# Routing steps of the second and third dense tile moved between the gate blocks of the tile in front

## The chip, the cores and the metric

The kernel runs on one core of a Trainium2 chip. The metric is the device time of one execution in microseconds (us). The engines named below are PE (TensorE, matrix products), DVE (VectorE), ACT (ScalarE), POOL (GpSimd, which here issues the gathers of table rows) and SP (SyncE, which issues the other transfers). Each engine runs its own list of instructions strictly in order; an instruction that has to wait for another engine or for a transfer holds up everything that is queued behind it on its engine.

## What is computed

One decoder layer on 512 tokens of width 1024: convolution and differential attention side by side, an output projection, then an expert layer ("peer"), then a gated per-layer embedding and a last norm. The change is in the expert layer, which for every token scores 128 + 128 keys in each of 8 heads, keeps the 16 best pairs, and mixes the 128 experts that these pairs name out of 16384:

```python
s = einsum('thcd,cnd->thcn', q, keys)
sv, si = top_k(s, 16)                       # per head and half
cand = sv[:, :, 0, :, None] + sv[:, :, 1, None, :]
cs, ci = top_k(cand.reshape(T, 8, 256), 16)
e1 = take_along_axis(si[:, :, 0], ci // 16); e2 = take_along_axis(si[:, :, 1], ci % 16)
experts, gates = e1 * 128 + e2, softmax(cs)
u = u_tab[experts]; h = gelu(einsum('cd,ckd->ck', x, u)) * gates
y = einsum('ck,ckd->cd', h, v_tab[experts])
```

## The kernel before

The 512 tokens are four tiles of 128. Three of them (the dense tiles, t = 0, 1, 2; `NA` = 3) compute all 16384 experts and multiply by a matrix of gates that is zero where an expert was not chosen. The fourth tile (the sparse tile) gathers its 128 u rows and then its 128 v rows per token from memory.

**Ups.** The dense tiles need u for 128 chunks of 128 experts. `up(c)` (L595) loads a chunk, splits it into a high part (`uhi`, ACT, L600) and a low part (`ulo`, a subtraction on DVE, L601; the first four on POOL), runs 24 matmuls (L67 to L69) and applies gelu (`av`, ACT). The third matmul of an up is the first that needs `ulo`. `more(n)` issues the next n ups. Ups are counted from 0 here; "up 48" is the 49th.

**Routing of a dense tile.** `pairs` (L504) finds the 16 best pairs of four heads, on DVE; it is called twice for a tile. `decode` (L515) turns them into two expert coordinates (one pass of the loop over c each) and the gates (`ef`). `decodeA` (L554) then transposes `ef` on PE (L558) and copies it on ACT (L559 to L562, the last is `gTH`) and DVE (`gTL`, L563).

**Gate blocks.** For every 16 tokens of a dense tile one block (L672 to L705) builds one-hot matrices on DVE (`o1` L690, on ACT in every third block; `eq2` L694; `o2` L695 and L696), multiplies them on PE (32 matmuls, L702) and copies the result out on ACT (`stage`, L704). Eight blocks make a tile. After every second block the gates are written to memory (`g_spill`).

**Rows.** `sparse(i)` (L573) gathers row i for each token of the sparse tile (a POOL issue, L576, 512 KB) into one of four buffers (`row`, L571), and DVE multiplies and sums it (L579). The DVE instruction is kept in program order. After 32 rows ACT applies gelu (`bh`, L582) and DVE multiplies by the gates (L583). `rows(n)` issues the next n.

**Order.** The program text gives the ups, rows and blocks in the order of the loop at L663: for each dense tile first two calls of `pairs` with two rows after each, then `decodeA`, two rows, four ups, then eight times three ups (`PER`), four rows (`ROWS`) and a block. A scheduler then reorders instructions on each engine by its own forecast, except those that are kept in program order. What is left over of the ups and rows is done in the last loop (L801), which runs the products with v (`down`, L740) for 128 chunks.

Of the kernel before, what the change touches and what calls it, by code (L numbers as in the profile page):

```python
# [10 lines left out]
F32 = mybir.dt.float32  # L11
# [15 lines left out]
NH, NK, TOPK = 8, 128, 16  # L27
HC = 2 * NH
NA = 3
# [7 lines left out]
HG = 4  # L37
WARM = 12
MIX = 2
EMB = 8  # L40
FIRST, PER = 16, 3
ROWS, POOLED = 4, 4
ACT_EVERY = 3
GS = 16384.0
# [10 lines left out]
def hymba_layer(ctx: ExitStack, tc: tile.TileContext, I, out):  # L55
# [270 lines left out]
    for i in range(len(units) + MIX + 1):  # L326
        if i < len(units):
            h, t = units[i]
# [5 lines left out]
        if 0 <= i - MIX - 1:  # L334
            h, t = units[i - MIX - 1]
# [134 lines left out]
    rbp = tc.alloc_tile_pool(name="rbp", bufs=1, side="right", reuse_waits="tile")  # L470
# [10 lines left out]
    setA, setB = store(rt, NA), store(rbp, 1)  # L481
# [30 lines left out]
        for j in range(HG):  # L512
            top16(cand[:, j], cs[:, t, h + j], ci[:, t, h + j], NCAND)

    def decode(st, t):  # L515
        sv, si, cs, ci = st
        ef = rbp.tile([128, 3, NH * TOPK], F32, name="ef")
        s16 = rbp.tile([128, 2, TOPK, NH], F16, name="s16")
        V.tensor_copy(s16, si[:, t].rearrange("p h c j -> p c j h"))
        late, fa, fb = (rbp.tile([128, TOPK, NH], F32, name="dc%d" % i) for i in range(3))  # L520
        iu = rbp.tile([128, NH, TOPK], U32, name="iu")
        iv = iu.rearrange("p h k -> p k h")
        V.tensor_scalar(late, ci[:, t].rearrange("p h k -> p k h"), float(NC0), None, op0=OP.is_ge)
        for c in range(2):
            if c == 0:
                V.tensor_scalar(iu, ci[:, t], 4, None, op0=OP.logical_shift_right)
                V.tensor_copy(fa, iv)
                V.tensor_scalar(iu, ci[:, t], 2, None, op0=OP.logical_shift_right)
                V.scalar_tensor_tensor(fb, iv, -12.0, fa, op0=OP.add, op1=OP.subtract)
            else:  # L530
                V.tensor_scalar(iu, ci[:, t], 15, None, op0=OP.bitwise_and)
                V.tensor_copy(fa, iv)
                V.tensor_scalar(iu, ci[:, t], 3, None, op0=OP.bitwise_and)
                V.tensor_tensor(fb, iv, fa, op=OP.subtract)
            V.tensor_tensor(fb, fb, late, op=OP.mult)
            fi = rbp.tile([128, TOPK, NH], F16, name="fi")
            V.tensor_tensor(fi, fa, fb, op=OP.add)
            eq = rbp.tile([128, TOPK, TOPK, NH], F16, name="eq")
            ev = eq.rearrange("p j k h -> p j (k h)")
            V.tensor_tensor(ev, jrep, fi.rearrange("p k h -> p (k h)")[:, None, :].to_broadcast([128, TOPK, 128]), op=OP.is_equal)  # L540
            V.tensor_tensor(eq, eq, s16[:, c][:, :, None, :].to_broadcast([128, TOPK, TOPK, NH]), op=OP.mult)
            for n in (8, 4, 2):
                V.tensor_tensor(ev[:, 0:n], ev[:, 0:n], ev[:, n:2 * n], op=OP.add)
            V.tensor_tensor(ef[:, c], ev[:, 0], ev[:, 1], op=OP.add)
        gt = rbp.tile([128, NH, TOPK], F32, name="gts")
        V.tensor_tensor(gt, cs[:, t], cs[:, t, :, 0:1].to_broadcast([128, NH, TOPK]), op=OP.subtract)
        A.activation(gt, gt, AF.Exp)
        gs = rbp.tile([128, NH], F32, name="gs")
        V.tensor_reduce(gs, gt, axis=AX.X, op=OP.add)
        V.reciprocal(gs, gs)  # L550
        V.tensor_tensor(ef[:, 2].rearrange("p (k h) -> p h k", h=NH), gt, gs[:, :, None].to_broadcast([128, NH, TOPK]), op=OP.mult)
        return ef

    def decodeA(t):  # L554
        ef = decode(setA, t)
        tp = rbank()
        for c in range(3):
            T.transpose(tp[:, c * 128:c * 128 + 128], ef[:, c], ident)  # L558
        A.activation(ne1[:, t], tp[:, 0:128], AF.Copy, scale=-1.0)  # L559
        A.activation(e1T[:, t], tp[:, 0:128], AF.Copy)  # L560
        A.activation(e2T[:, t], tp[:, 128:256], AF.Copy)
        A.activation(gTH[:, t], tp[:, 256:384], AF.Copy, scale=GS)  # L562
        V.scalar_tensor_tensor(gTL[:, t], tp[:, 256:384], GS, gTH[:, t], op0=OP.mult, op1=OP.subtract)  # L563

    def routeB():
        ef = decode(setB, 0)
        V.tensor_copy(bgate, ef[:, 2])
        V.scalar_tensor_tensor(bidx, ef[:, 0], float(NK), ef[:, 1], op0=OP.mult, op1=OP.add)

# [57 lines left out]
    def more(n):  # L627
        nonlocal nu
        while n > 0 and nu < EARLY:
            up(first[nu])  # L630
            nu += 1
            n -= 1
# [21 lines left out]
    def rows(n):  # L654
        nonlocal nxt
        while n > 0 and nxt < 128:
            sparse(nxt)
            nxt += 1
            n -= 1

    routeB()
    more(FIRST)
    for t in range(NA):  # L663
        for h in range(0, NH, HG):
            pairs(setA, t, h)
            rows(2)
        decodeA(t)
        rows(2)
        more(4)
        for b in range(128 // GT):  # L670
            stage = gst.tile([128, NK, GT], F32, name="stage")
            for g in range(GT // GB):  # L672
                tk = b * GT + g * GB
                more(PER)
                rows(ROWS)
                sh = [128, GB // 2, 128, 2]

# [251 lines left out]
```

## Time and profile before

| what | value |
|---|---|
| median of 3 runs | 1567.97 us (1564.33 to 1573.69) |
| the profiled execution | 1570.4 us, its span 1568.6 us |
| mean granted clock of TensorE | 0.983 |
| PE busy | 1505.2 us (96%) |
| DVE busy | 1248.0 us (80%) |
| ACT busy | 719.7 us (46%) |
| POOL busy | 465.7 us (30%) |

The profile gives each instruction's start and duration, and for an engine that sat idle what ended the idle time. Routing, ups and gate blocks run from about 367 us to 879 us of the span; what comes before (attention and convolution) and most of what comes after (the products with v) is not touched. The durations of neighbours on DVE overlap a little, so for a sum the distance from one start to the next is what counts.

### The profile page before, as it was taken

The numbers are of one execution on the slowest core, as the hardware profiler recorded it, in microseconds if no ns is written. First come the engines' busy times: TensorE is split into PE (matmuls) and PEld (weight loads), VectorE is DVE, ScalarE is ACT, GpSimd is POOL, SyncE is SP. The second block draws the span as 40 slices with busy tenths as digits, with TensorE's granted clock in tenths as the row PEclk, the third lists the DMA queues.
The fourth block names the chain that finished last, engine by engine and source line by source line (L and its number), as shares of the span: only waits on it lengthen the run. The fifth ranks groups of instructions, "written<-read, shape, count | busy, mean of one in ns | idle before, by whom it ended". The sixth has DMA issues, their size and how long they took to land. (4 is left out here: it accounts for less than half of the span.)

```text
span 1568.6 us, 22429 instructions
## 1 busy us (share of the span) xinstructions
PE 1505.2 (96%) x7929; PEld 1315.7 (84%) x7929; DVE 1248.0 (80%) x2411; ACT 719.7 (46%) x1133; POOL 465.7 (30%) x316
## 2 busy tenths in 40 slices
PE   8989898999999999999999999999999999998997
PEld 6867476889999989999999878888888888876786
DVE  4999863789999999988884677878788787768756
ACT  5434664223347764776666433333333333334433
POOL 0000103331223444344442234433344453432000
PEclk9999998999999999999999999999999999999999
DMA  7232245311779999999999999999998898989612
GB/s 238 94 109 54 81 161 204 107 55 41 256 211 347 336 339 335 349 400 373 363 366 361 351 345 332 329 328 329 332 338 328 308 326 307 325 325 329 232 40 81
DMA packets 148689, 410.31 MB, mean 262 GB/s; under 512 B 15072, under 2 KB 66144, under 8 KB 147040
## 3 DMA queue, kind: packets, MB, share of 16 engines
q1 hardware_dynamic: 111136, 272.55, 49.9%
q0 software_dynamic: 36864, 134.23, 22.8%
q10 hardware_dynamic: 576, 2.10, 0.3%
q8 instruction: 62, 1.02, 0.3%
q14 instruction: 51, 0.42, 0.1%
HBM read 355.41 MB, written 51.31 MB: 259 GB/s over the span
## 5 line engine op out<-in xcount | busy, mean ns | idle before, releaser
L576 POOL DMA_INDIRECT row<-in_v,bidx x128 | 214.8, 1678 | 300.8 <-DVE acc L587 285.1
L576 POOL DMA_INDIRECT row<-in_u,bidx x128 | 193.8, 1514 | 345.4 <-DVE row L579 301.0
L69 PE MATMUL ups<-mTH,ulo 128*128 128x384 f32 x760 | 256.7, 338 | 2.3 <-DVE ulo L601 2.2
L67 PE MATMUL ups<-mTH,uhi 128*128 128x384 f32 x760 | 257.9, 339 | 0.3 <-ACT av L607 0.3
L68 PE MATMUL ups<-mTL,uhi 128*128 128x384 f32 x760 | 256.3, 337 | 0.0
L740 PE MATMUL y<-vlo,hH 128*128 128x512 f32 x768 | 238.5, 392 | 11.2 <-DVE vlo L64 11.2
L600 ACT ACTIVATE uhi<-uraw 128x1024 fp32r<-128x1024 f32 x128 | 135.2, 1060 | 229.3 <-PE ups L68 157.0
L740 PE MATMUL y<-vhi,hH 128*128 128x512 f32 x768 | 237.9, 391 | 2.3 <-ACT vhi L63 2.3
L740 PE MATMUL y<-vhi,hL 128*128 128x512 f32 x768 | 237.6, 391 | 0.0
L63 ACT ACTIVATE hH<-hf 128x384 fp32r<-128x384 f32 x128 | 67.1, 524 | 288.9 <-PE y L740 215.9
L601 DVE TENSOR_TENSOR ulo<-uraw,uhi 128x1024 fp32r<-128x1024 f32 x124 | 150.8, 1221 | 44.0 <-ACT uhi L600 40.8
L740 PEld LDWEIGHTS y<-vlo,hH 128*128 128x128 f32 x768 | 143.6, 188 | 45.6 <-DVE vlo L64 15.7
L579 DVE SCALAR_TENSOR_TENSOR row<-row,mB 128x1024 f32<-128x1024 f32 x128 | 152.4, 1223 | 25.2 <-DMA row<-in_u,bidx 25.0
L740 PEld LDWEIGHTS y<-vhi,hH 128*128 128x128 f32 x768 | 143.7, 188 | 32.3 <-ACT vhi L63 4.0
L740 PEld LDWEIGHTS y<-vhi,hL 128*128 128x128 f32 x768 | 144.7, 188 | 30.3
L587 DVE SCALAR_TENSOR_TENSOR acc<-row,bh,acc 128x1024 f32<-128x1024 f32 x127 | 162.5, 1279 | 0.0
L64 DVE TENSOR_TENSOR hL<-hf,hH 128x384 fp32r<-128x384 f32 x128 | 71.3, 557 | 112.8 <-ACT hH L63 112.8
L64 DVE TENSOR_TENSOR vlo<-vraw,vhi 128x1024 fp32r<-128x1024 f32 x128 | 156.2, 1220 | 5.3 <-ACT vhi L63 5.3
L69 PEld LDWEIGHTS ups<-mTH,ulo 128*128 128x128 f32 x760 | 142.6, 188 | 3.7 <-DVE ulo L601 3.6
L67 PEld LDWEIGHTS ups<-mTH,uhi 128*128 128x128 f32 x760 | 142.7, 188 | 1.4 <-ACT av L607 0.6
L68 PEld LDWEIGHTS ups<-mTL,uhi 128*128 128x128 f32 x760 | 142.7, 188 | 1.0
L63 ACT ACTIVATE vhi<-vraw 128x1024 fp32r<-128x1024 f32 x128 | 135.6, 1059 | 15.8 <-DMA vraw<-in_v 15.3
(276 smaller groups left out, 2613.5 us busy)
## 6 DMA issues: line engine op xcount, KB each, us to landing
uraw<-in_ut SPq DMA_DIRECT2D x128, 512.0 KB, 6.6
vraw<-in_v SPq DMA_DIRECT2D x128, 512.0 KB, 5.5
g_spill<-stage SPq DMA_DIRECT2D x12, 2048.0 KB, 10.4
gt<-g_spill SPq DMA_DIRECT2D x16, 1536.0 KB, 11.5
a_spill<-av SPq DMA_DIRECT2D x101, 192.0 KB, 6.8
ga<-a_spill SPq DMA_DIRECT2D x101, 192.0 KB, 6.9
qraw<-in_wq SPq DMA_DIRECT2D x16, 512.0 KB, 3.8
wraw<-in_w_in SPq DMA_DIRECT2D x15, 512.0 KB, 4.1
```

The lines of the kernel that those rows point to most:

```text
L63: A.activation(hi, src, AF.Copy)
L64: V.tensor_tensor(lo, src, f32(hi), op=OP.subtract)
L67: T.matmul(ps, wh, xh, start=first, stop=False)
L68: T.matmul(ps, wh, xl, start=False, stop=False)
L69: T.matmul(ps, wl, xh, start=False, stop=last)
L576: P.indirect_dma_start(out=row, out_offset=None, in_=I["u"] if i < 128 else I["v"], in_offset=bass.IndirectOffsetOnAxis(ap=bidx[:, j:j + 1 ...
L579: tc.keep_in_program_order(V.scalar_tensor_tensor(row, row, 1.0, mB, op0=OP.mult, op1=OP.mult, accum_out=ba[:, j:j + 1]))
L587: tc.keep_in_program_order(V.scalar_tensor_tensor(acc, row, bh[:, j:j + 1], acc, op0=OP.mult, op1=OP.add))
L600: A.activation(hi, raw, AF.Copy)
L601: (P if c in first[:POOLED] else V).tensor_tensor(lo, raw, f32(hi), op=OP.subtract)
L740: T.matmul(y[t][n], w[:, sl], x[:, n * 512:n * 512 + 512], start=c == 0 and w is hH and x is hi, stop=c == NK - 1 and l)
```

## The change

The routing of a dense tile becomes a generator, `routeA`, that stops after each call of `pairs`, after each of the two coordinates, and after the gates; its last step is the transposes and copies. That makes six steps. The routing of tile 0 still runs as a whole before the first block, now with two rows and one up (`CHORE_UPS`) at each of its five stops. The routing of tile t + 1 is stepped once in each of the first six blocks of tile t, behind the three ups of the block and ahead of its four rows; in the last two blocks nothing is left to step. Ahead of tile 1 and tile 2 stand four ups and no rows; ahead of tile 0 the four ups are gone (five were issued at the stops).

```diff
+CHORE_UPS = 1
...
-    def decode(st, t):
+    def decode(st, t, ef):
         sv, si, cs, ci = st
-        ef = rbp.tile([128, 3, NH * TOPK], F32, name="ef")
...
             V.tensor_tensor(ef[:, c], ev[:, 0], ev[:, 1], op=OP.add)
+            yield
...
-        return ef
-
-    def decodeA(t):
-        ef = decode(setA, t)
+        yield
+
+    def new_ef():
+        return rbp.tile([128, 3, NH * TOPK], F32, name="ef")
+
+    def routeA(t, paired=False):
+        for h in range(0, 0 if paired else NH, HG):
+            pairs(setA, t, h)
+            yield
+        ef = new_ef()
+        yield from decode(setA, t, ef)
         tp = rbank()
...
     def routeB():
-        ef = decode(setB, 0)
+        ef = new_ef()
+        for _ in decode(setB, 0, ef):
+            pass
...
     routeB()
     more(FIRST)
+    chores = routeA(0)
     for t in range(NA):
-        for h in range(0, NH, HG):
-            pairs(setA, t, h)
+        for _ in chores:
             rows(2)
-        decodeA(t)
-        rows(2)
-        more(4)
+            more(CHORE_UPS)
+        if t:
+            more(4)
+        chores = routeA(t + 1) if t + 1 < NA else iter(())
         for b in range(128 // GT):
             stage = gst.tile([128, NK, GT], F32, name="stage")
             for g in range(GT // GB):
                 tk = b * GT + g * GB
                 more(PER)
+                next(chores, None)
                 rows(ROWS)
```

The lists of instructions that come out of the scheduler show where this lands. The line numbers of the changed kernel are 8 to 12 higher; `ulo` is the subtraction of an up, `row,ba` one gathered row.

DVE before, from the subtraction of up 43 on, while PE works on the last block of tile 0:

```order
L601 TENSOR_TENSOR ulo<-uraw,uhi 128x1024
L579 SCALAR_TENSOR_TENSOR row,ba<-row,mB 128x1024 x4
L498 MAX_INDEX ci<-cs,tscr 128x8
L494 MAX cs<-cand 128x8
L579 SCALAR_TENSOR_TENSOR row,ba<-row,mB 128x1024
L601 TENSOR_TENSOR ulo<-uraw,uhi 128x1024
L579 SCALAR_TENSOR_TENSOR row,ba<-row,mB 128x1024 x2
L601 TENSOR_TENSOR ulo<-uraw,uhi 128x1024
L579 SCALAR_TENSOR_TENSOR row,ba<-row,mB 128x1024
```

Here eight rows stand close together, numbers 34 to 41. The rows 30 to 33 stand ten and more microseconds of DVE work ahead of them, and the instruction `gTL` of tile 1 follows only behind up 46.

DVE after, from `gTL` of tile 1 on, which now stands behind the subtraction of up 41:

```order
L571 SCALAR_TENSOR_TENSOR gTL<-rbank,gTH 128x128
L589 SCALAR_TENSOR_TENSOR row,ba<-row,mB 128x1024 x2
L702 TENSOR_TENSOR o_5488<-irep,e1T 128x2048
L593 TENSOR_TENSOR bh<-bh,bgate 128x32
L589 SCALAR_TENSOR_TENSOR row,ba<-row,mB 128x1024 x4
L611 TENSOR_TENSOR ulo<-uraw,uhi 128x1024
L589 SCALAR_TENSOR_TENSOR row,ba<-row,mB 128x1024 x2
L611 TENSOR_TENSOR ulo<-uraw,uhi 128x1024
L707 TENSOR_TENSOR o_5491<-eq_5490,gTH 128x2048
L611 TENSOR_TENSOR ulo<-uraw,uhi 128x1024
L589 SCALAR_TENSOR_TENSOR row,ba<-row,mB 128x1024 x4
L708 TENSOR_TENSOR o_5491<-eq_5490,gTL 128x2048
```

One more subtraction and four more rows follow: rows 30 to 45, sixteen of them, now stand between the subtractions of up 41 and up 46, and none stands between up 35 and up 41.

ACT before, at the copies of the transposed `ef` of tile 1 (L559 to L562); `stage` is the copy out of a gate block, here the last of tile 0:

```order
L600 ACTIVATE uhi<-uraw 128x1024
L607 ACTIVATE av<-ups 128x384
L704 ACTIVATE stage<-rbank 128x4x128 x4
L559 ACTIVATE ne_2154<-rbank 128x128
L560 ACTIVATE e1T<-rbank 128x128
L561 ACTIVATE e2T<-rbank 128x128
L562 ACTIVATE gTH<-rbank 128x128
```

ACT after, at the same copies:

```order
L610 ACTIVATE uhi<-uraw 128x1024
L617 ACTIVATE av<-rbank 128x384
L567 ACTIVATE ne_2154<-rbank 128x128
L568 ACTIVATE e1T<-rbank 128x128
L569 ACTIVATE e2T<-rbank 128x128
L570 ACTIVATE gTH<-rbank 128x128
L716 ACTIVATE stage<-rbank 128x4x128 x4
L592 ACTIVATE bh<-ba 128x32
L610 ACTIVATE uhi<-uraw 128x1024
```

The copies moved from behind the eighth block of tile 0 to ahead of its sixth, five ups earlier, and the gelu of the first 32 row products (`bh`) follows the copies of that block at once.

## Rows read from the trace of the kernel before

**Rows 1.** Busy time by stretch; columns PE, PEld, DVE, ACT, POOL, PEclk, DMA share, GB/s

```profile
560.00:580.00 20.00, 17.06 (x113) 16.57 (x114) 17.11 (x43) 14.05 (x25) 9.65 (x7) 0.95 0.96 348
580.00:600.00 20.00, 17.93 (x90) 17.61 (x89) 19.83 (x43) 11.80 (x20) 6.69 (x5) 0.88 1.00 388
...
375.00:600.00 225.00, 214.95 (x1370) 210.08 (x1369) 215.24 (x520) 128.91 (x196) 70.47 (x48) 0.98 0.82 288
600.00:860.00 260.00, 260.00 (x1830) 257.46 (x1829) 216.28 (x272) 174.30 (x265) 107.55 (x70) 1.00 0.97 362
860.00:935.00 75.00, 70.77 (x336) 61.63 (x336) 49.46 (x73) 27.34 (x39) 23.55 (x15) 0.98 0.98 361
...
1100.00:1200.00 100.00, 100.00 (x463) 85.59 (x462) 78.61 (x91) 37.34 (x50) 41.89 (x25) 1.00 0.93 335
```

**Rows 2.** PE's waits from 375 to 620 us: total us, times, longest

```profile
PE rbank L69 <- DVE ulo L601: 7.8, 6, 2.9
PE ups L69 <- DVE ulo L601: 2.2, 3, 0.9
```

**Rows 3.** PE in order of time: start, us, what, idle before

```profile
428.70 0.44 PE L69 MATMUL rbank<-mTH,ulo 128*128 128x384 f32 x1 [1.30 <-DVE ulo L601]
466.40 2.01 PE L702 MATMUL rbank<-o,o 128*128 128x128 f16 x32
468.22 0.42 PE L67 MATMUL rbank<-mTH,uhi 128*128 128x384 f32 x1
578.12 0.69 PE L69 MATMUL rbank<-mTH,ulo 128*128 128x384 f32 x1 [2.92 <-DVE ulo L601]
594.59 0.44 PE L69 MATMUL rbank<-mTH,ulo 128*128 128x384 f32 x1 [2.07 <-DVE ulo L601]
600.43 0.33 PE L69 MATMUL ups<-mTH,ulo 128*128 128x384 f32 x1
604.59 0.33 PE L69 MATMUL ups<-mTH,ulo 128*128 128x384 f32 x1
```

**Rows 4.** DVE in order of time, from up 14 to up 48

```profile
427.43 1.21 DVE L601 TENSOR_TENSOR ulo<-uraw,uhi 128x1024 fp32r<-128x1024 f32 x1
508.56 1.23 DVE L579 SCALAR_TENSOR_TENSOR row<-row,mB 128x1024 f32<-128x1024 f32 x1 [2.05 <-DMA row<-in_u,bidx]
543.50 1.22 DVE L601 TENSOR_TENSOR ulo<-uraw,uhi 128x1024 fp32r<-128x1024 f32 x1
544.63 1.22 DVE L695 TENSOR_TENSOR o<-eq,gTH 128x2048 f16<-128x2048 f16 x1
545.77 1.22 DVE L696 TENSOR_TENSOR o<-eq,gTL 128x2048 f16<-128x2048 f16 x1
568.21 1.22 DVE L579 SCALAR_TENSOR_TENSOR row<-row,mB 128x1024 f32<-128x1024 f32 x1
569.36 1.22 DVE L579 SCALAR_TENSOR_TENSOR row<-row,mB 128x1024 f32<-128x1024 f32 x1
575.69 1.23 DVE L579 SCALAR_TENSOR_TENSOR row<-row,mB 128x1024 f32<-128x1024 f32 x1 [2.38 <-DMA row<-in_u,bidx]
598.99 1.22 DVE L601 TENSOR_TENSOR ulo<-uraw,uhi 128x1024 fp32r<-128x1024 f32 x1
```

**Rows 5.** POOL in order of time: the issues of four gathers

```profile
569.71 1.68 POOL L576 DMA_INDIRECT row<-in_u,bidx  x1 [7.79 <-DVE row L579]
571.69 1.99 POOL L576 DMA_INDIRECT row<-in_u,bidx  x1 [0.30 <-issue]
573.99 0.93 POOL L576 DMA_INDIRECT row<-in_u,bidx  x1 [0.30 <-issue]
```

**Rows 6.** The tile `row` from 400 to 600 us: gathers from issue to landing

```profile
DMA to landing us min/median/max: 5.1/8.0/11.1
```

**Rows 7.** PE in order of time: the last gate block, the first product with v

```profile
847.04 1.96 PE L702 MATMUL rbank<-o,o 128*128 128x128 f16 x32
878.58 0.63 PE L740 MATMUL y<-vhi,hH 128*128 128x512 f32 x2
```

**Rows 8.** ACT and DVE in order of time: the first two parts of v

```profile
871.88 1.06 ACT L63 ACTIVATE vhi<-vraw 128x1024 fp32r<-128x1024 f32 x1 [1.91 <-DMA vraw<-in_v]
873.22 1.22 DVE L64 TENSOR_TENSOR vlo<-vraw,vhi 128x1024 fp32r<-128x1024 f32 x1
```

## The prediction

> **What bounds the kernel now.** I read the busy times by stretch first. From 600 to 860 us PE is busy all of the time and its clock is full: there the ups and gate blocks run back to back, and no rearrangement can win anything. From 375 to 600 us PE is idle for 10 of 225 us while DVE is busy for 215 [rows 1]. The list of PE's waits says for what: nine times for `ulo`, the subtraction of an up on DVE, 10.0 us in all [rows 2]. So in this stretch, and only there, DVE is the late one: routing of all three tiles, one-hot matrices, rows and subtractions come to more than PE's own work. The two largest waits, 2.92 and 2.07 us, stand at the border between tile 0 and tile 1 [rows 3].
>
> That lag can be counted. At up 14 PE has just waited for DVE (428.70, subtraction at 427.43), and at up 48 the two meet again (600.43, subtraction at 598.99) [rows 3, 4]. Between them PE has 34 ups and 8 blocks. An up is 4.16 us (600.43 to 604.59), a block 1.82 (466.40 to 468.22) [rows 3]: with 0.6 for six transposes 156.8 us. It took 171.7, so it lost 14.9; that is more than the idle time in its list, because in the last 40 us it also ran at a granted clock of 0.95 and 0.88 [rows 1], which cost nothing of its own, since DVE set the pace. DVE between the same two points has 34 subtractions (1.13 from start to start), 40 rows (1.145), 35 one-hot instructions (1.135) [rows 4]; that is 38.4 + 45.8 + 39.7. Its list of waits in between is six waits for a gathered row, of which 2.05 and 2.38 are the longest [rows 4] and which sum to 6.95, and about 1.8 us in small pieces, 8.7 in all. What is left of its 171.6 us is 38.9 for the short routing instructions. So the loss of 14.9 is 6.1 of DVE work in excess of PE's work (162.8 against 156.8), and 8.7 in which DVE itself stood waiting, nearly all of it for rows. Everything that the change can do here is in these two terms. From about 605 us on PE is never behind again before the products with v begin.
>
> **The change, part by part.**
>
> *Amount of work.* Nothing is added: the same instructions, moved. The rows issued in the tile loop are 10 + 3 x 32 = 106 instead of 3 x (6 + 32) = 114; eight rows go to the last loop. There each is 1.145 us of a DVE that is busy for 78.61 of 100 us while PE is full [rows 1], so they hide. If that cover were gone they would cost 9 us.
>
> *The first term, DVE's excess.* The scheduler had already put much of tile 1's and tile 2's routing between the blocks of the tile in front, so the step-wise text moves less than it says. I add up the list of the changed kernel with the same distances from start to start, again from up 14, up to which both lists are alike. Up to up 42: 28 subtractions, 32 rows, 28 one-hots, 33.7 of routing, 133.7 us against 130.0 of PE (28 ups, 7 blocks): excess 3.8. Up to up 52, where it is largest: 42.9 + 52.7 + 43.1 + 41.5 = 180.3 against 175.2 (38 ups, 9 blocks): 5.0. Up to up 59: 50.9 + 65.3 + 49.9 + 46.5 = 212.6 against 208.1: 4.5. The excess is thus 1.1 us below the 6.1 of before. That is the whole direct gain.
>
> *The second term, DVE's waits for rows.* Rows have four buffers. In a run of rows the fifth can be fetched only when DVE has freed the first. Before: the first row of a run at 568.21 was done when the next began at 569.36, POOL issued the next gather at 569.71, and the row that used it began at 575.69 after a wait of 2.38 us [rows 4, 5], 6.0 us from issue to use. Over the stretch a gather takes 5.1 to 11.1 us, median 8.0 [rows 6]; POOL's next issue follows after 0.93 to 1.99 us plus 0.30 [rows 5]. Before, the longest run was eight rows. Now the rows of block six are held behind `gTL` of tile 1, which waits in program order ahead of them, and the list shows sixteen (rows 30 to 45) between up 41 and up 46, with none in the five ups ahead. Up to the start of the last there are fifteen rows, four subtractions and three one-hots to do, 17.2 + 4.5 + 3.4 and `bh` with 0.1: 25.2 us. The gathers set: 1.5 us to free and issue the first, then eleven more at a spacing of 1.3 to 2.3, then the landing of 6 to 9. With 1.6 and 6 the last is there at 25.1, and only the fifth row waits: four rows, a one-hot and `bh` end at 5.8, the gather at 1.5 + 6, a wait of 1.7 us; with 2.3 and 9 at 35.8, a wait of 10.6. In between, 2.1 and 8 give 32.6 - 25.2 = 7.4; I take 7, nearest to the median landing. Two smaller runs: rows 22 to 29 around up 33 (0 to 4, I take 2) and rows 54 to 60 around up 58 (0 to 3.6, I take 2.5). The small pieces stay at 1.8. So the waits are 10.8 up to up 52 and 13.3 up to up 59, where before they were 8.7.
>
> *The lag then.* At up 52: 5.0 + 10.8 = 15.8. At up 59: 4.5 + 13.3 = 17.8. PE's loss is the largest of these, 17.8, against 14.9: 2.9 us more. With all waits at their low ends (1.7 + 1.8) it is 8.5, a gain of 6.4; with all at their high ends (10.6 + 4 + 3.6 + 1.8 = 20.0) it is 24.5, a loss of 9.6.
>
> *New waits in order.* PE's transposes of tile 1 now stand ahead of its sixth block and want the gates of `decode`; by the same sums DVE is done with these some 20 us before PE gets there, so PE doesn't wait. `gTL` on DVE waits for the copies on ACT; DVE comes there after PE's transposes, since it is the late engine. On ACT the gelu `bh` waits for row 31 and has the `uhi` of up 42 behind it; DVE wants that only after four more rows. I cost all three at nothing; the cover is DVE's lag itself, and without it the first would cost up to 1.8, a block.
>
> *The passage to v.* One up more is issued ahead of the first block, so one fewer (six, not seven) stands between the last block and the first product with v. In that time the last gates go to memory and back. Before, `vhi` was done at 872.94 and `vlo` at 874.44, and PE began at 878.58 [rows 7, 8]: 5.6 and 4.6 us of slack (`vlo` is wanted 0.4 later). An up is 4.16 [rows 3], so 1.5 and 0.4 are left. I take 1 us, from 0 to 3: the transfers of this stretch run at a share of 0.98 [rows 1].
>
> **Sum.** 2.9 + 1 is 3.9 us on the profiled execution's 1570.4, so about 1574.3; the median of the runs shown is 1567.97, and on that base 1572.
>
> **The rivals.**
>
> *The burst costs what the slower gathers say.* If the sixteen rows run at POOL's longer spacing of 2.3 and landings of 9 us and more, the loss is 9.6, with the passage up to 12.6: 1578 to 1581. For it: landings up to 11.1 were seen [rows 6]. Against it: while DVE stands, no other buffers come free and other transfers pause too, and in the burst of before the landing was down to 6.0. It decides from waits of 15 us up to up 59. The Trainium skill (SBUF — State Buffer, section "A bandwidth-pool intuition that's wrong") says that a gather's descriptors can be locked out by a DVE instruction on the shared port, and that an issue of about 0.62 us then takes about 3.1; by that figure, an estimate, eleven issues would add some 9 us more and the time would be near 1590. The issues of this trace take 0.93 and 1.99, so it bears out a slow-down with a busy DVE, but not that size.
>
> *The rows land in time.* If the run is fed at 1.6 us and 6 us, as in the best part of the burst of before, DVE's waits shrink to 3.5, PE's loss is 8.5, and the time is 1562; if the small pieces of 1.8 go too, the loss is 6.7 and the time 1560, and lower only if the passage to v wins as well, some 4 us at most, 1556. For it: rows are spread more evenly at the start of tile 0 (14 instead of 6 by up 21), and the eight-row run at the border is gone. Against it: the list shows a longer run, not a shorter one.
>
> *It does nothing.* The scheduler had hoisted the routing already; then excess and waits trade evenly and the time stays at 1568. This lies inside the forecast's own range, 1563 to 1576.
>
> **How the numbers follow.** 0.5% is 7.8 us, about what a measurement of this kernel can tell from no change: below 1560 is faster, above 1576 slower. Forecast and "does nothing" together have 0.44, all of it within 0.5%. The slow burst has 0.36. The rows in time have 0.20, of which 0.06 lie above 1560 and 0.14 below, since my sums can be off by the few us that part the two. That makes 0.14 faster, 0.50 the same, 0.36 slower. The range reaches up to the end of the slow burst and down to where the fast case leaves it: 1560 to 1582.
>
> **What will show it.** Right: PE's waits for `ulo` still end by about 630 us and come to a loss of 16 to 20 from up 14 on; DVE's waits for rows between up 41 and up 46 are 5 to 9 us, larger than any group before; PE full from 640 to 860; 106 rows done before the first v product. Wrong: PE waiting at the transposes or at a block (L702 before, L714 after); waits for rows below 4 us (then faster); a wait of over 3 us ahead of the first product with v; or a change in the stretch after 935 us, where I expect none.

## The result, and the profile after

The changed kernel takes 1579.45 us (median of 6 runs, 1574.05 to 1582.46) and the kernel before, timed beside it, 1568.89 us (6 runs, 1564.16 to 1573.69). The ratio is 1.0071 with a 95% interval of 1.005 to 1.0092: slower by 0.7%, 10.6 us. The profiled execution took 1579.0 us with a span of 1577.2, 8.6 us over that of before. That lies in the range given (1560 to 1582) and at the time that the rival "the burst costs what the slower gathers say" had (1578 to 1581), not at the forecast. By the prediction's own lines (above 1576 is slower) it is the slower case, to which it gave 0.36, and not the same, to which it gave 0.50.

Busy time by stretch in the profile after (columns as in [rows 1]):

```profile
375.00:600.00 225.00, 212.01 (x1360) 208.65 (x1359) 210.42 (x500) 124.84 (x192) 70.40 (x50) 0.98 0.82 284
600.00:860.00 260.00, 250.62 (x1725) 246.60 (x1724) 205.87 (x262) 168.26 (x258) 94.81 (x59) 0.98 0.89 327
860.00:935.00 75.00, 72.89 (x396) 66.50 (x395) 45.16 (x64) 31.37 (x42) 18.88 (x13) 1.00 0.99 359
560.00:580.00 20.00, 14.55 (x96) 14.08 (x96) 11.86 (x18) 13.10 (x26) 10.02 (x8) 0.83 0.95 340
580.00:600.00 20.00, 17.86 (x124) 17.26 (x123) 18.70 (x37) 9.54 (x12) 8.64 (x6) 1.00 0.98 347
```

The second line is the surprise. From 600 to 860 us PE was busy for all of 260.00 us before [rows 1]; now it is idle for 9.4 of them, at a granted clock of 0.98. The PE waits of the changed kernel, first from 375 to 620 us (total us, times, longest), where [rows 2] has those of before, then from 640 to 860 us, where before had none:

```profile
PE ups L70 <- DVE ulo L611: 8.4, 6, 5.5
PE rbank L714 <- DVE o L708: 2.9, 3, 1.1
PE rbank L714 <- DVE o L707: 2.2, 1, 2.2
PE rbank L70 <- DVE ulo L611: 0.2, 1, 0.2
```

```profile
PE rbank L70 <- DVE ulo L611: 5.1, 1, 5.1
PE ups L70 <- DVE ulo L611: 3.0, 1, 3.0
PE rbank L714 <- DVE o L708: 0.3, 1, 0.3
```

PE still waits for `ulo`, but in a few long stalls of 5.5, 5.1 and 3.0 us, where before the longest was 2.9 [rows 2]. It also waits at gate blocks for one-hot matrices (L707, L708), which it didn't before. PE in order of time, with the matmuls behind the first stall and, last, the first product with v:

```profile
529.69 0.23 PE L714 MATMUL rbank<-o,o 128*128 128x128 f16 x1 [2.23 <-DVE o L707]
...
569.24 0.69 PE L70 MATMUL ups<-mTH,ulo 128*128 128x384 f32 x1 [5.45 <-DVE ulo L611]
569.73 0.52 PE L68 MATMUL ups<-mTH,uhi 128*128 128x384 f32 x1
570.05 0.52 PE L69 MATMUL ups<-mTL,uhi 128*128 128x384 f32 x1
...
572.79 0.34 PE L69 MATMUL ups<-mTL,uhi 128*128 128x384 f32 x1
572.96 0.33 PE L70 MATMUL ups<-mTH,ulo 128*128 128x384 f32 x1
...
659.03 0.69 PE L70 MATMUL rbank<-mTH,ulo 128*128 128x384 f32 x1 [5.11 <-DVE ulo L611]
...
718.50 0.44 PE L70 MATMUL ups<-mTH,ulo 128*128 128x384 f32 x1 [2.97 <-DVE ulo L611]
...
892.41 0.62 PE L752 MATMUL y<-vhi,hH 128*128 128x512 f32 x2
```

The first product with v starts at 892.41, where before it started at 878.58 [rows 7]: 13.8 us late. What DVE did while PE stood is seen in its own order of time:

```profile
554.03 0.28 DVE L571 SCALAR_TENSOR_TENSOR gTL<-rbank,gTH 128x128 f16<-128x128 f32 x1
554.23 1.21 DVE L589 SCALAR_TENSOR_TENSOR row<-row,mB 128x1024 f32<-128x1024 f32 x1
...
565.28 1.23 DVE L589 SCALAR_TENSOR_TENSOR row<-row,mB 128x1024 f32<-128x1024 f32 x1 [5.16 <-DMA row<-in_u,bidx]
...
580.06 1.23 DVE L589 SCALAR_TENSOR_TENSOR row<-row,mB 128x1024 f32<-128x1024 f32 x1 [2.09 <-DMA row<-in_u,bidx]
...
651.87 1.23 DVE L589 SCALAR_TENSOR_TENSOR row<-row,mB 128x1024 f32<-128x1024 f32 x1 [3.25 <-DMA row<-in_u,bidx]
...
716.07 1.22 DVE L589 SCALAR_TENSOR_TENSOR row<-row,mB 128x1024 f32<-128x1024 f32 x1 [6.28 <-DMA row<-in_u,bidx]
```

Each long stall of PE (569.24, 659.03, 718.50) comes just behind a long wait of DVE for a gathered row (565.28, 651.87, 716.07). POOL's issues show why the first is so long:

```profile
555.72 1.68 POOL L586 DMA_INDIRECT row<-in_u,bidx  x1 [26.75 <-DVE row L589]
557.71 0.95 POOL L586 DMA_INDIRECT row<-in_u,bidx  x1 [0.31 <-issue]
...
566.79 0.94 POOL L586 DMA_INDIRECT row<-in_u,bidx  x1 [4.62 <-DVE row L589]
```

POOL had stood for 26.75 us, because all four buffers were full while the rows waited in program order behind `gTL`. The first row ran at 554.23, the next gather was issued at 555.72, and the row that used it began at 565.28, 9.6 us later; in the burst of before that took 6.0 us [rows 4, 5]. A POOL that stands costs nothing by itself: in e1 and e9 below it stands for 29.01 us (up to 611.28) and 27.04 us (up to 600.77), and PE has no long stall there: the rows behind it come four at a time, with the subtractions of three ups between, and DVE is ahead. DVE's waits for rows from 375 to 860 us, before and then after, show the same thing in one line each:

```profile
DVE row L579 <- DMA row<-in_u,bidx: 25.0, 25, 2.4
```

```profile
DVE row L589 <- DMA row<-in_u,bidx: 32.8, 20, 6.3
```

The total grew by only 7.8 us, but fewer waits carry it and the longest is 6.3 us in place of 2.4.

**The ledger.** As in the prediction, PE's loss is the time from up 14 to a later up less PE's own work between them. It is read from one profiled execution of each kernel. Before it was 15.0 us at up 48 and then crept to 16.4 at up 76 and 18.3 at up 106. After it is 7.5 at up 36, 15.2 at up 43, 19.7 at up 52, 28.0 at up 60, 33.1 at up 71, 33.6 at up 76 and 35.2 at up 106: 16.9 us more. Up 14 came 3.0 us earlier than before (425.67 against 428.70), which leaves the 13.8 us at the first product with v. From there to the end of the span it took 684.8 us against 690.0, so 5.2 us came back, and 8.6 us of span remain.

### The profile page after: what moved, and what is told of

The parts are those of the page before. It is cut to its first block, busy times and chain, and to the rows that moved or that the text cites. A ratio compares the mean times of both kernels' runs of the same rounds, so it can differ in the third digit from the quotient of the medians.

```text
span 1577.2 us, 22429 instructions
## 1 busy us (share of the span) xinstructions
PE 1507.6 (96%) x7929; PEld 1319.9 (84%) x7929; DVE 1247.1 (79%) x2411; ACT 719.3 (46%) x1133; POOL 453.6 (29%) x316
## 5 line engine op out<-in xcount | busy, mean ns | idle before, releaser
L586 POOL DMA_INDIRECT row<-in_v,bidx x128 | 205.2, 1603 | 280.0 <-DVE acc L597 261.2
```

Source lines behind the costliest of these rows:

```text
L586: P.indirect_dma_start(out=row, out_offset=None, in_=I["u"] if i < 128 else I["v"], in_offset=bass.IndirectOffsetOnAxis(ap=bidx[:, j:j + 1 ...
```

## The experiments

Theory 1: rows that are held in program order behind the routing step of their block come in runs longer than their four buffers. DVE then stands for gathers, and PE for DVE. Theory 2: six steps of routing are simply too dense in six blocks (and five in front of tile 0), so that DVE's work is late without any gather. All numbers of a loss below are from up 14 to up 76; "rest" is the span from the first product with v on. The medians are of 4 to 10 runs. Each group of four was timed beside the kernel before once more (1567.31 us for e1 to e4, 1568.02 for e5 to e8, 1568.50 for e9 to e12), so the ratio is the fairer number between groups. The last three columns are of one profiled execution, which can lie some us off the median: 4.3 above it in e1, 3.8 above in e7, 2.7 below in e8, 3.1 below in e9. The kernels e3 and e4 leave out the gathers of u, so what they compute for the sparse tile isn't the layer's.

| kernel | median us | ratio to before (95%) | loss | first product with v | rest |
|---|---|---|---|---|---|
| before | 1568.89 | | 16.4 | 878.58 | 690.0 |
| after | 1579.45 | 1.0071 (1.005 to 1.0092) | 33.6 | 892.41 | 684.8 |
| e1 step behind the rows | 1565.27 | 0.9988 (0.9974 to 1.0001) | 15.2 | 878.54 | 689.3 |
| e2 last step between tiles | 1567.54 | 0.9996 (0.9979 to 1.0013) | 21.7 | 881.89 | 686.1 |
| e3 before, no u gathers | 1550.97 | 0.9893 (0.9863 to 0.9922) | 7.6 | 864.88 | 683.3 |
| e4 after, no u gathers | 1550.88 | 0.9899 (0.9865 to 0.9933) | 10.3 | 866.38 | 680.2 |
| e5 start alone | 1581.59 | 1.0074 (1.0054 to 1.0094) | 26.2 | 888.37 | 691.2 |
| e6 blocks alone | 1590.63 | 1.0139 (1.0115 to 1.0163) | 41.0 | 898.23 | 690.1 |
| e7 e1, fewer rows in tile 0 | 1573.06 | 1.0029 (1.0014 to 1.0044) | 7.7 | 868.86 | 706.1 |
| e8 before, fewer rows in tile 0 | 1572.12 | 1.0028 (1.0014 to 1.0043) | 15.4 | 873.07 | 694.5 |
| e9 e6, step behind the rows | 1563.56 | 0.9967 (0.9957 to 0.9977) | 10.2 | 870.37 | 688.3 |
| e10 four buffers of raw u | 1589.69 | 1.013 (1.0095 to 1.0165) | 33.8 | 895.49 | 690.4 |
| e11 e10, five row buffers | 1585.46 | 1.011 (1.0076 to 1.0144) | 35.3 | 893.15 | 691.6 |
| e12 e11, step behind the rows | 1565.23 | 0.998 (0.9968 to 0.9992) | 11.6 | 870.22 | 695.3 |

**e1: the step behind the rows.** Two lines change places.

```diff
-                next(chores, None)
                 rows(ROWS)
+                next(chores, None)
```

> The changed kernel with one swap: in a gate block the four rows are issued ahead of the routing step, not behind it. Theory 1 (rows held behind gTL come in runs longer than their four buffers, DVE waits for gathers, PE for DVE): the list now has no run above four rows without three ups between, so the DVE waits for rows between up 41 and up 46 (10.0 us) and at up 58 (5.5) nearly vanish; PE's loss from up 14 to up 76 falls from 33.6 to 9 to 14 us, and the time from 1579.5 to 1558 to 1566, below the kernel before. Theory 2 (the routing itself is too dense in six blocks, so that one-hot matrices and subtractions are late whatever the rows do): the same routing stands in the same blocks, so the time stays at 1575 to 1582.

The loss fell from 33.6 to 15.2 us and the time by 14 us (13 by the ratios), to that of before or slightly under it. DVE's waits for rows from 375 to 860 us:

```profile
DVE row L589 <- DMA row<-in_u,bidx: 14.8, 16, 3.0
```

So the same steps in the same blocks cost nothing over the kernel before once the rows don't stand behind them: theory 2 can't explain the slowdown. The late step itself hardly moved: `gTL` of tile 1 runs at 559.02 here and at 554.03 in the changed kernel. The loss is 1 us above the span expected for it (9 to 14), because the start takes 6.5 us up to up 24, where the routing of tile 0 with its rows and ups is most crowded. The changed kernel, whose first rows stand behind a step, has a loss of 1.3 us there.

**e2: only the last step moved.** The transposes and gate copies of tiles 1 and 2 are done between the tiles, the other five steps as after.

```diff
         if t:
+            for _ in chores:
+                pass
             more(4)
...
-                next(chores, None)
+                if b * (GT // GB) + g < 5:
+                    next(chores, None)
```

> The changed kernel, but only five steps in the blocks; the sixth (transposes, copies, gTL) runs between the tiles, ahead of the four ups. Theory 1: rows 30 to 37 are no longer held by gTL, but rows 38 to 47 still stand together at the border; the waits at up 42 and at up 70 go, that at up 59 (rows 54 to 61) stays: 1566 to 1573. Theory 2: five of six steps are where they were, 1575 to 1582.

The stalls at ups 42 and 70, behind `gTL`, are gone; the loss at up 36, where a gate block waits 2.9 us, and a wait of 3.3 us at up 59 remain. So about 12 of the 17 us of added loss hang on the last step alone.

**e3 and e4: no gathers of u.** DVE's instructions stay as many and as long; POOL issues nothing for these rows.

```diff
+        if i >= 128:
             P.indirect_dma_start(out=row, ...)
         if i < 128:
-            tc.keep_in_program_order(V.scalar_tensor_tensor(row, row, 1.0, mB, ...))
+            tc.keep_in_program_order(V.scalar_tensor_tensor(row, mB, 1.0, mB, ...))
```

> The kernel before without the 128 gathers of u rows; the DVE instruction on a row stays, and reads a tile that is there anyway (the sums of the sparse tile are then not those of the layer). Theory 1: PE's loss between up 14 and up 48 is then DVE's excess alone, 6.1 plus up to 1.8 instead of 14.9, and the time 1558 to 1563. Theory 2: rows matter little, 1565 to 1570.

> The changed kernel, likewise without the gathers of u rows and with the same DVE work. Theory 1: its excess is 5.0, so the loss up to up 76 falls from 33.6 to 5 to 8 us and the time to 1552 to 1560, no slower than the kernel before without gathers (within 4 us of it). Theory 2: the distance of about 11 us between the two kernels stays: 1568 to 1574.

The two are equal as far as four runs of each tell: 1550.97 and 1550.88, with intervals of about 5 us to either side. With DVE's work left as it was, the 10.6 us between before and after are gone, so they come from the gathers. In the loss 2.7 us are left (10.3 against 7.6), which takes e4 out of its 5 to 8. The runs also check the first term. Without gathers the loss of before is 5.9 us at up 48, where the prediction had 6.1 of excess. After, one stall is left, and it is where the sum had 3.8 us of excess, at up 42. PE of e4 in order of time:

```profile
558.51 0.69 PE L70 MATMUL ups<-mTH,ulo 128*128 128x384 f32 x1 [3.45 <-DVE ulo L612]
```

Behind it the loss goes from 6.0 us at up 42 to 8.7 an up later without a wait, because eighteen matmuls follow at 0.32 us: that is the 2.7 us. That e3 came out 7 us below its range, and e4 1 us below its own, can have two sources that these runs don't part: the rest of the span is shorter too (683.3 and 680.2 us), and there are fewer transfers.

**e5 and e6: each part alone.** In e5 tile 0 has its five stops with rows and ups, and tiles 1 and 2 are routed as a whole between the tiles; in e6 tile 0 is routed as a whole, with its six rows and four ups behind it, and the steps stand in the blocks as after.

```diff
 (e5)
         if t:
+            for i, _ in enumerate(routeA(t)):
+                rows(2 if i in (0, 1, 4) else 0)
             more(4)
-        chores = routeA(t + 1) if t + 1 < NA else iter(())
+        chores = iter(())
 (e6)
         for _ in chores:
-            rows(2)
-            more(CHORE_UPS)
-        if t:
-            more(4)
+            pass
+        if t == 0:
+            rows(6)
+        more(4)
```

> One part of the change alone: tile 0 is routed with two rows and one up at each of five stops, but tile 1 and tile 2 are routed as a whole between the tiles, as before. Theory 1 (runs of rows behind gTL): rows 30 to 37 stand in two groups again, the long run (38 to 47) is at the border as before; PE's loss from up 14 to up 76 is 14 to 18 us, like the 16.4 of before and not the 33.6 of the change: 1563 to 1571. Theory 2 (rows crowded into the start of tile 0 are what costs): most of the change's loss stays, 1574 to 1580.

> The other part alone: tile 0 is routed as a whole before its first block (its six rows and four ups behind it, as one group), and tile 1 and 2 in six steps in the blocks, as in the change. Theory 1: rows 26 to 41 stand together behind gTL of tile 1, sixteen as in the change, and rows 58 to 69 behind that of tile 2: loss 28 to 36 us, time 1575 to 1582. Theory 2: without the crowded start the time is that of the kernel before, 1564 to 1572.

I missed with e5: 1581.59 for an expected 1563 to 1571. The second theory of that run, that the rows crowded into the start are what costs, had 1574 to 1580 and came nearer. It pays 6.5 us at ups 22 to 24, as e1 does, and then again at the border between tiles 0 and 1, in four waits between ups 45 and 52, and at the next border. PE in order of time:

```profile
463.95 0.69 PE L70 MATMUL ups<-mTH,ulo 128*128 128x384 f32 x1 [2.13 <-DVE ulo L611]
...
593.55 0.64 PE L70 MATMUL rbank<-mTH,ulo 128*128 128x384 f32 x1 [3.33 <-DVE ulo L611]
...
616.79 0.44 PE L70 MATMUL ups<-mTH,ulo 128*128 128x384 f32 x1 [2.40 <-DVE ulo L611]
```

The border has ten rows in a run (38 to 47) and an excess of 7.0 us by the sum of its order, more than the 6.1 of before. Spreading the start alone is thus not free, which I had held it to be: with tiles 1 and 2 routed between the tiles it costs some 10 us, without any wait of DVE for a row above 2.5 us. e6 missed upwards, with a loss of 41.0 for 28 to 36 and 1590.63 for 1575 to 1582. It shows the stalls of after, two of the three longer, in PE's and then DVE's order of time:

```profile
567.77 0.69 PE L70 MATMUL rbank<-mTH,ulo 128*128 128x384 f32 x1 [6.46 <-DVE ulo L611]
...
659.21 0.69 PE L70 MATMUL ups<-mTH,ulo 128*128 128x384 f32 x1 [7.58 <-DVE ulo L611]
...
718.14 0.44 PE L70 MATMUL ups<-mTH,ulo 128*128 128x384 f32 x1 [2.10 <-DVE ulo L611]
```

```profile
652.52 1.23 DVE L589 SCALAR_TENSOR_TENSOR row<-row,mB 128x1024 f32<-128x1024 f32 x1 [6.16 <-DMA row<-in_u,bidx]
```

So the steps in the blocks carry the mechanism, and they are worse (1.0139) without the new start. Part of that is the same thing once more at tile 0: its `gTL` stands at 437.55, rows 0 to 9 come behind it, DVE waits 5.4 us for gathers among them, and the loss is 5.3 us at up 24. The two parts don't add up: their losses exceed that of before by 9.8 and 24.6 us, and both together by 17.2.

**e7 and e8: fewer rows early.** In the first tile two rows stand in a block, not four; the rest goes to the loop of the products with v. e7 does it in e1, e8 in the kernel before.

```diff
-                rows(ROWS)
+                rows(ROWS if t else 2)
```

> The swap of the first experiment (rows ahead of the routing step), and two rows instead of four in each block of tile 0; the sixteen rows go to the last loop, where DVE is busy for four fifths of the time. Theory 1: both terms shrink, DVE's excess to 2.7 at up 22 and below 2 elsewhere, and no wait for rows where DVE is late; loss 3 to 7 us where the swap alone had 15.2, time 1552 to 1560, faster than both kernels. If instead the last loop can't take sixteen rows more (transfers there run at a share of 0.9 and more), the gain is given back and the time is 1563 to 1568.

> The kernel before with two rows instead of four in each block of tile 0 and nothing of the change. Theory 1: DVE's excess in tile 0 is at most 2.3, the longest run six rows where DVE has time; loss 3 to 7 us instead of 16.4, time 1553 to 1561. It tells whether the change is of any use beside it: if this is as fast as the run with the swap and two rows, the step-wise routing brings nothing of its own.

In e7 the loss fell to 7.7, just above what was expected (3 to 7), and the first product with v came at 868.86; then the rest of the span took 706.1 us, 17 more than in e1. PE's waits from 860 us on, before and then e7:

```profile
PE y L740 <- DVE vlo L64: 11.2, 9, 2.4
PE y L740 <- ACT vhi L63: 2.3, 3, 1.0
```

```profile
PE y L752 <- ACT vhi L64: 9.3, 3, 6.2
PE y L752 <- DVE vlo L65: 8.5, 4, 6.1
PE y L752 <- ACT hH L64: 5.0, 1, 5.0
```

The stalls moved: PE now waits for v and h. The time of e7, 1573.06, is above both ranges that I gave (1552 to 1560, and 1563 to 1568 if the last loop can't take the rows): I had held that this loop hides sixteen more rows as it hides eight. e8 missed in the loss itself, 15.4 for 3 to 7; its rest is 4.5 us longer. Fewer rows didn't mean fewer waits there. DVE's waits for rows of e8 from 375 to 860 us, and the longest:

```profile
DVE row L579 <- DMA row<-in_u,bidx: 34.5, 26, 5.2
```

```profile
555.51 1.23 DVE L579 SCALAR_TENSOR_TENSOR row<-row,mB 128x1024 f32<-128x1024 f32 x1 [5.22 <-DMA row<-in_u,bidx]
```

PE stalls for 2.82 us just behind it, at up 42. As a test of the change beside fewer rows the two come out even (1.0028 and 1.0029): with these rows the step-wise routing gains 7.7 us in the loss and nothing in the time.

**e9: blocks alone, step behind the rows.** e6 with the two lines of e1 exchanged. It has neither the crowded start nor the long runs.

> Edit: tile 0 is routed whole ahead of its blocks, as before the change, and the steps of tiles 1 and 2 stand in the blocks, but behind the four rows of their block. It takes both excesses out that the earlier runs showed: the 6.4 us at ups 22 to 24 that the rows-first form pays for its crowded start, and the long runs behind the turned gates that the blocks-alone form pays for (41.0 us of loss to up 76). The DVE work ahead of each ulo, summed over this order, exceeds PE's by 2.5 us at up 19 and by 6.4 us at up 49. Theory 1 (runs of rows behind the turned gates make the waits): no run of more than six rows is left, so the waits for rows stay as in the rows-first form (5 us in all) and the loss to up 76 is 8 to 13 us; no PE wait over 2 us at ups 35, 41, 58 or 69, where the blocks-alone form had its stalls of 4.8, 6.5, 7.6 and 2.1 us. Median 1560 to 1567, if the products with v take 689 to 692 us as in the other forms with as many rows behind; two to four rows more are left behind than in the rows-first form, which can cost 2 to 4 us there. Theory 2 (six steps crowded into the blocks are the cost): the loss stays near that of the blocks alone, 1585 to 1592.

This has the lowest median of the versions that compute the whole layer: 1563.56 us, ratio 0.9967 (0.9957 to 0.9977), 4.9 us under the kernel before as timed beside it (1568.5) and some 16 under the changed one. The intervals of e1 and e12 overlap with it. The loss is 10.2 us, as expected, against 41.0 in e6: 31 us from the exchange of two lines, and `gTL` of tile 1 runs at 549.44 where in e6 it ran at 552.71. PE's waits from 400 to 800 us, DVE's for rows from 375 to 860, and the busy times of two stretches (columns as in [rows 1]):

```profile
PE ups L70 <- DVE ulo L611: 2.4, 3, 1.9
PE rbank L70 <- DVE ulo L611: 1.2, 1, 1.2
PE rbank L714 <- DVE o L708: 1.2, 1, 1.2
```

```profile
DVE row L589 <- DMA row<-in_u,bidx: 21.5, 22, 3.7
```

```profile
400.00:600.00 200.00, 195.25 (x1278) 192.20 (x1277) 195.88 (x443) 120.92 (x186) 61.53 (x41) 1.00 0.86 301
600.00:860.00 260.00, 259.77 (x1825) 256.70 (x1824) 197.04 (x238) 174.23 (x265) 95.72 (x64) 1.00 0.96 352
```

The 5 us that I had named for DVE's waits are what e1 has from up 14 to up 52 (of its 14.8 from 375 to 860). Here the five up to there, all ahead of 600 us, come to 3.9 us. The 17.6 us behind 600 don't matter, since DVE's summed work is ahead of PE's again: at 612.75 DVE waits 3.7 us for a row and PE doesn't stall. It is the length of a single wait against DVE's lead that counts, not the total.

**e10, e11, e12: a fifth row buffer.** It needs room, which one buffer of raw u gives; e10 is the control with that alone, e12 the same buffers with the step behind the rows.

```diff
 (e10, e11, e12)
-        raw = urp.tile([128, KT, 128], F32, name="uraw", bufs=5)
+        raw = urp.tile([128, KT, 128], F32, name="uraw", bufs=4)
 (e11, e12)
-        return gp.tile([128, D], F32, name="row", bufs=4)
+        return gp.tile([128, D], F32, name="row", bufs=5)
```

> Edit: the changed kernel with four buffers of raw u in place of five, nothing else: the control of the next run, which needs their room. Four buffers shorten the lead of the loads of u. Median between that of the changed kernel, 1579, and 15 us more; the waits for rows as in the changed kernel (32.8 us from 375 to 860) within 4 us by either theory.

> Edit: the changed kernel with four buffers of raw u and five row buffers in place of four. Theory 1 (in a long run of rows the gathers set the pace: four in flight at about 8 us a landing give one row in 2.0 us, against 1.23 us that the operation of a row takes): five in flight give one in 1.6 us, so about half of the excess per row goes, and one more row is ready when a run begins: over the run of 16 rows 10 us of waits become about 4 to 5, over those of 8 to 12 rows 4 to 6 us become 1 to 3. Waits for rows from 375 to 860 fall from 32.8 us to 15 to 22, and the median is 5 to 12 us below the run with four buffers of raw u and four of rows. If landings grow longer with one more in flight, so that the bytes per time stay the same, the waits fall by one row's time a run only, 1 to 3 us in all. Theory 2 (dense steps): within 2 us of the control.

> Edit: the changed kernel with the step of each block behind its four rows, and four buffers of raw u with five of rows. Theory 1: with the long runs gone already (waits for rows of 5 us in all in the rows-first form), a fifth buffer has little left to take: within 3 us of the rows-first form (1565.3) plus what the control loses by four buffers of raw u. A gain of more than 4 us against that would say that gathers still set the pace in runs of four to six rows.

Four buffers of raw u cost about 10 us by themselves. The loss up to up 76 has no part in that (33.8, as in the changed kernel 33.6): of the 8.7 us in the span 5.6 lie in the rest, and up 14 came 2.6 late. The fifth row buffer gives at most a few us back: the intervals of e10 and e11 overlap, and the loss didn't fall (35.3). DVE's waits for rows went from 34.0 to 27.6 us, not to 15 to 22. The run behind `gTL` of tile 1 in e11, on POOL and on DVE:

```profile
551.98 1.68 POOL L586 DMA_INDIRECT row<-in_u,bidx  x1 [26.78 <-DVE row L589]
```

```profile
555.17 1.22 DVE L589 SCALAR_TENSOR_TENSOR row<-row,mB 128x1024 f32<-128x1024 f32 x1
...
561.42 1.23 DVE L589 SCALAR_TENSOR_TENSOR row<-row,mB 128x1024 f32<-128x1024 f32 x1 [5.03 <-DMA row<-in_u,bidx]
```

Five rows were ready now, and still DVE waited 5.03 us, because the first new gather starts only when the run does (551.98) and needs 9.4 us. One row of 1.15 us more was there, but the scheduler had taken a one-hot instruction of about the same length out from between them, and it put eight rows ahead of the subtraction of up 42 where it had put six. So this pair isn't a clean test of the buffers: the order changed with them. e12 is as fast as e1 (1565.23 against 1565.27) although its control costs 10 us: its loss is 3.6 us smaller, its waits for rows are 4.4 us instead of 14.8, and up 14 came 4.7 us earlier, but its rest is 6.0 longer. By the expectation's own bound this would say that gathers set the pace in runs of four to six rows as well. It isn't shown: the 10 us are those of the other order, and e1 with four buffers of raw u and four of rows wasn't run.

## Why the prediction came out as it did

**Right: what bounds the stretch and where.** PE waits for `ulo`, DVE for gathers, from up 14 on; both terms, and the place behind `gTL` of tile 1, are as told. The first term holds in its size (5.9 measured in e3 for 6.1; a stall of 3.45 in e4 where 3.8 was summed). The gain of 1.1 us that was read from it doesn't show: e4 has a loss of 9.0 us at up 48, 2.7 of it from the clock behind its stall. (By its own prices PE's work up to up 48 is 156.6 us, not 156.8, and the loss of before 15.1; nothing hangs on that.) The direction of 2.9 us more was right, and so were the waits of the rival that priced them high: it was to decide from 15 us of waits up to up 59, and there were 20.8. With all waits at their high ends the prediction had a loss of 24.5 us at up 59, and it is 25.3.

**Luck: that the time lies in the range.** The loss in the whole stretch is 16.9 us more than before, where the worst case that I had priced was 9.6, and 12.6 with the passage to v. That the time still fell at 1579 is owed to two things that the prediction doesn't have: up 14 came 3.0 us earlier, and the rest was 5.2 us shorter. Without them it would have been some 1588 us, an estimate (1579.45 + 8.2), beyond the range.

**Wrong: the size of the second term.** I took the middle of each bound. The waits of the run of sixteen rows, from up 41 to 46, are 9.45 us (5.16, 0.25, 0.71, 2.09, 0.63 and 0.61), for which I took 7 (1.7 to 10.6); rows 22 to 29 have 3.5 (2.60 and 0.93) for 2 (0 to 4); rows 54 to 60 have 5.5 (3.25, 0.98, 1.29) for 2.5, above the upper bound of 3.6. With 2.3 in small pieces that is 20.8 at up 59, where I had 13.3: 7.5 us. The choice failed in the landings. I took the median of 8.0 us [rows 6] and argued that a standing DVE makes gathers faster. The first gather of the run took 9.6 us from issue to use, with the DMA engines at a share of 0.95 from 560 to 580, the others that DVE waited for 8.4 to 9.5 except the last (6.0), and those of rows 58 to 60 took 9.8 to 10.3.

**Wrong: two costs that weren't in the sum.** The first is a third place, the rows behind `gTL` of tile 2. I had DVE ahead there by the sum of its work. It isn't ahead without bound. `uhi` and `ulo` have three buffers each, so ACT writes the next `uhi` only when PE has left the oldest, and DVE waits for ACT, 29.2 us in all from 375 to 860:

```profile
DVE ulo L611 <- ACT uhi L610: 29.2, 14, 4.0
```

From up 63 to up 69 the subtraction ends at most 8.25 us before PE wants it (up 69: 701.09 and 709.34), some two ups. The waits of 1.36 and 6.28 us for rows ate that, and PE stalled for 2.97. With the clock behind it that is 4.9 us. The second is the clock. I wrote that the lower clock of before cost nothing, since DVE set the pace; that holds only where DVE is late again at once. After the stall at 569.24 PE's matmuls start every 0.32 us, and from 572.79 on every 0.17: the lower of the two levels (1.2 GHz) and then the full one (2.4). From 560 to 580 the granted clock is 0.83, where it was 0.95 before [rows 1]. DVE was soon ahead again, so this was PE's own time: the loss goes from 13.6 at up 42 to 15.2 an up later, and from 25.3 at up 59 to 28.0 an up later, with no wait shown. The first of the two is swallowed when DVE is late again (25.3 at up 59 is DVE's excess of 4.5 and its waits of 20.8), the second stays. Of the 14.0 us by which the loss at up 106 exceeds the predicted 2.9, the waits carry 7.5, the clock at up 59 2.7, the third place 4.9; smaller pieces of both signs, 1.1 in all, go the other way.

**The passage to v.** I took 1 us, from 0 to 3. PE had no wait ahead of the first product with v. The term is nil, and the 13.8 us at that point are the loss less the 3.0 us by which up 14 came early.

**Given back.** The rest of the span was 5.2 us shorter, where I expected no change; PE's waits for `vlo` from 860 us on are 4.8 us instead of 11.2. e1, with as many rows left over, has 689.3, like before. The rest of the kernels with all gathers and four rows a block lies between 684.8 and 695.3, and executions of the kernel before lie up to 9.5 us apart, so this can be the way the phases happen to fall. What sets it stays open.

**The signs that I named.** 106 rows were done in the tile loop, and PE didn't wait at the transposes. DVE's waits between up 41 and up 46, 9.45 us, are just above the 5 to 9. An end of PE's waits by 630 us, a loss of 16 to 20, and PE full from 640 to 860 us: all wrong, by the stalls at 659.03 and 718.50. Waiting at a block, which I had named as a sign against the theory: it occurred, 5.1 us in all up to 620 us, as a side effect of the same late DVE. The Trainium skill (SBUF — State Buffer, section "A bandwidth-pool intuition that's wrong") has a DMA issued from GpSimd at about 3.1 us beside a copy on DVE, for want of descriptors, and at about 0.62 alone; the prediction took these for times of an issue. So read, the sixteen issues from 540 to 600 us lie between the two, at 0.94 to 1.98 us, median 1.56, and none comes near 3.1. What was slow here was the landing, not the issue. A single issue of e6 was far slower, beside a DVE that worked throughout; no row came late by it:

```profile
495.54 9.22 POOL L586 DMA_INDIRECT row<-in_u,bidx  x1 [0.30 <-issue]
```

**What is shown and what is not.** Shown: without gathers the difference is gone (e3, e4), and with the rows ahead of the step it is gone as well (e1, e6 against e9). Not shown: why the new start alone costs 9.8 us of loss in e5 and hardly any in the change. Only argued: that the landings of 8 to 10 us are long because of the other transfers. That more buffers would cure it is not shown either, since e11's order changed with them.

## What to carry to other kernels

Work that waits for transfers shouldn't stand in program order behind a step that comes late: while the step waits, the buffers are full and nothing is fetched, and when it is through, the whole latency falls on one place. Put such work ahead of the late step, a buffer's worth at a time; two exchanged lines were worth some 13 us in one kernel here and 27 in another (by the ratios). When you sum an engine's lag, cap its lead by the buffers between the engines, price the gathers of a burst at the slow end of the landings seen, and add the clock behind each long stall of PE where PE is not held up again at once.

## What the runs showed of the hardware that I had not expected

- After a PE wait of 5.11 us eighteen matmuls started at a distance of 0.32 us instead of 0.17, which cost 2.7 us on top of the wait; after 5.45 us it was ten, for 1.6 us. The price doesn't grow with the wait: 9.10 us in e11 were followed by seventeen such matmuls (2.6 us), 2.07 us in the kernel before by eleven (1.5 us), and 2.22 us in e1 by none to speak of (0.1 us). The kernel e9 has no wait over 1.9 us from 400 to 800 us, and a granted clock of 1.00 from 400 to 860.
- Sixteen rows more in the loop of the products with v went with a longer rest, by 17 us in e7 (over e1) and 4.5 in e8 (over before; one execution each), though DVE is busy for only 78.61 of 100 us there [rows 1]. An engine with a fifth of its time free in the mean didn't hide them.
